# The end of the column projections of a hybrid decoder step: order of work by a readiness clock, key tiles of 256 rows, copies between partition halves

## The chip, the cores and the metric

One core of a Trainium2 chip runs the whole program. The metric is the device time of one execution in microseconds (us); the runs of a version are summed up by their median. Five engines take part, each with its own queue of instructions: TensorE (PE: matmuls and transposes; PEld is its weight load), VectorE (DVE), ScalarE (ACT), GpSimd (POOL) and SyncE (SP), which here issues nearly all DMA transfers. An engine takes its instructions in the order of its queue and waits at an instruction whose inputs or buffers are not ready.

## The reference

One layer of a decoder over a prompt of 1024 rows of width 1024, and one new row for each of 8 samples. One projection feeds three groups of heads, which are gated, joined and projected back:

```python
q_raw, kv_raw, g_raw, z_nsa, u_rw, z_rw, q_mem, z_mem = split_in(rms_norm(hp, ln_g[l]) @ w_in[l])
q, rows4, rows_w = nsa_project(q_raw, kv_raw, pos_p, nsa_q_norm[l], nsa_k_norm[l])
gates = jax.nn.sigmoid(g_raw).reshape(bp, tp, NSA_HEADS, 3)
o_nsa = lax.map(lambda a: nsa_prompt_seq(*a, *cmp_params), (q, rows4, rows_w, gates))
o_rw, sh_p, st_p = rwkv7_mix(u_rw, ...)          # a recurrence over the rows: state S, output y
mkv_p = mem_kv(mem_prompt, mem_norm_g[l], w_mem_kv[l], mem_k_norm[l])   # rms_norm(mem) @ w_kv, 256 rows
o_mem = mem_attend(q_mem, mkv_p, mem_q_norm[l])
hp = hp + mixer_out(o_nsa, z_nsa, o_rw, z_rw, o_mem, z_mem, w_out[l])
```

`nsa_prompt_seq` attends to compressed blocks of keys (made by a small network, `compress`), to selected blocks and to a window, for 8 query heads and 2 key heads of 64. The samples do the same with cached rows. All of it is in float32.

## The kernel before

The program is written in Python that emits one instruction after another; a scheduler then puts every engine's instructions in an order of its own, by the order of emission as priority, by priorities raised with `high_priority`, and by its own model of times. Three tools bind that order. `issue_after(x)` puts an instruction behind x on x's engine. The class `InOrder` (line 72) issues each TensorE instruction after the one before it, so that TensorE's order is the order of emission, and keeps a `clock`, a sum of written costs (0.46 ns a column for a product of float32r, at least 256 columns; 0.11 us a transpose). Its products show up in the profile as line 86 (a helper's line). TensorE instructions on plain `nc.tensor` show their own lines and may be moved by the scheduler.

A float32 product is made of three matmuls, high part by high part, high by low, low by high (`project`, line 298): each weight block is loaded (`wraw`), split by ScalarE into `whi` and by VectorE into `wlo` (two buffers each).

Work before the attention (`phase1`, line 481):

- The columns of `w_in` come in tiles of 128 (`columns`, line 660). Each tile is projected for the rows 0 to 511 with the samples (pieces of 256 and 264) and for the rows 512 to 1023 (one piece of 512): 3 x 24 matmuls. `ORDER` sets their order, the first 17 (`EARLY`) are early columns, the last four are late ones, all of kind z: their result passes ScalarE (tanh) and VectorE (`do_z`, line 309) and is stored to `z_d` by SP.
- The recurrence runs in four chunks of 256 rows (`rwkv_prep`, `rwkv_state`, line 827). Its steps depend on each other; `drive` (line 597) emits as much of the early columns behind each step as the step's `yield` says, as a filler. In `rwkv_state` follow each other: p_x (products of the inverse), its copies W (ScalarE, line 927) and UV (VectorE, line 930), p_g for t = 0 and t = 1 with evictions PT and GT (lines 935 to 949), p_z and p_yy, four steps of p_z and Zn (line 971), and the last part of p_yy. At the end `rwkv_out` makes the rows y and SP stores them (`y_d`, line 1011); `rwkv_close` turns the last state (p_s, line 1017) and SP stores it (line 1021).
- Then `self.pe = nc.tensor`: the late columns are emitted (their matmuls show line 306) and after every 8 of their steps 8 steps of `ahead` (`BG`), which weaves two chains. `attn_keys` (line 1231) loads eight key tiles of 128 rows, each twice side by side (two DMAs of 128 KB, line 1236; the buffer `kd4` has `KB` = 2 turns), turns them by four transposes into PSUM (line 1242, p_k in the profile) and evicts high part (kh, ScalarE, line 1244) and low part (kl, VectorE, line 1245) over all 128 partitions: every key stands on both halves of the partitions, since a query's high part stands on one half and its low part on the other (`q_stack`, line 1292). The values `vs` are loaded in between (line 1238). The other chain is `prompt_cmp` (line 1247: constants, transposes p_xt, the network p_hid and p_co, the turn of the compressed key in `k_split`, line 1190), then `mem_kv` (line 1125): eight groups of two transposes p_mT with evictions mhi and mlo, then the product p_mo (line 1154) in four blocks of 12 matmuls of 512 columns, each with a load and split of `w_mem_kv`; norm and store of the memory's keys and values.

PSUM: the pool `ptr` has two banks (`pM` here), `pw` three, `ppr` three for the columns. `phase2` is the attention; its first scores are p_s<-kh,qs.

Of the kernel before, what the change touches and what calls it, by code (L numbers as in the profile page):

```python
# [26 lines left out]
KB = 2  # L27
# [3 lines left out]
BG = 8  # L31
# [82 lines left out]
class Step:  # L114
# [197 lines left out]
    def do_z(self, H, pieces, row):  # L312
# [6 lines left out]
        nc.sync.dma_start(self.z_d[row:row + 128, H * HALF:H * HALF + HALF], t[:, :HALF])  # L319
# [151 lines left out]
    def phase1(self):  # L471
# [8 lines left out]
        with ExitStack() as ctx:  # L480
# [91 lines left out]
            self.pe = nc.tensor  # L572
# [255 lines left out]
    def rwkv_state(self, Q):  # L828
# [103 lines left out]
        GT, PT = [None] * 2, [None] * 2  # L932
# [23 lines left out]
        yield 0.9  # L956
# [8 lines left out]
        for n in range(4):  # L965
            Zn = self.rc.tile([128, 2, 64], F32, name="Zn", tag="Z", bufs=5)
            for c in range(2):
                for h in range(2):
                    PE.matmul(pz[half[h], n, c, :], PT[n // 2][half[h], c, n % 2, :], Zs[n][half[h], c, :],
# [6 lines left out]
        for t in range(2):  # L976
            for c in range(2):
                for p, h in ((0, 0), (1, 1), (1, 0), (0, 1)):
                    PE.matmul(pyy[h][half[1 - p], t, c, :], GT[t][half[h], c, p, :], Zs[2 * t + p][half[h], c, :],
# [13 lines left out]
    def rwkv_out(self, Q, t, y, yb):  # L993
# [17 lines left out]
        nc.sync.dma_start(self.y_d[r0:r0 + 128, :], yf)  # L1011

    def rwkv_close(self):
        nc, O = self.nc, self.O
        ps = self.pw.tile([128, 2, 128], F32, name="p_s", tag="w")
        for c in range(2):
            nc.tensor.transpose(ps[:64, c, :], self.Z[:, c, :], self.ident[:])
# [15 lines left out]
    def cmp_consts(self):  # L1033

        nc, I = self.nc, self.I
        V, PE = nc.vector, nc.tensor
# [45 lines left out]
    def compress(self, xt, n, hid):  # L1082
# [4 lines left out]
        for e in range(2):  # L1087
# [10 lines left out]
            yield  # L1098

    def cmp_out(self, hid2):  # L1100
# [3 lines left out]
        nc.tensor.matmul(ps[:, :128], hid2, self.w2d[:].rearrange("p a b -> p (a b)"), start=True, stop=True)  # L1104
# [20 lines left out]
    def mem_kv(self):  # L1125
        nc, I, O = self.nc, self.I, self.O
        V, A, PE = nc.vector, nc.scalar, nc.tensor
        xs = self.mem_rows
        his = [self.slot(j, [128, 4, 256], F32R, f"mhi{j}") for j in (4, 0)]
        los = [self.slot(j, [128, 4, 256], F32R, f"mlo{j}") for j in (5, 1)]  # L1130
        for k in range(8):
            ps = self.pM.tile([128, 512], F32, name="p_mT", tag="m")
            for t in range(2):
                PE.transpose(ps[:, t * 128:(t + 1) * 128], xs[t][:, k * 128:(k + 1) * 128], self.ident[:])
            g = self.v("mem_norm_g", k)
# [1380 lines left out]
```

## Time and profile before

| | |
|---|---|
| median of 3 runs | 936.83 us (936.18 to 936.99) |
| the profiled execution | 936.7 us, span 934.9 us |
| TensorE busy | 899.3 us (96%) |
| VectorE, ScalarE, GpSimd busy | 648.0, 434.2, 178.7 us |
| granted clock of TensorE, mean | 0.998 |
| chain that ended last | PE 73%, DVE 17%, ACT 5%, DMA 2%, issue 2% |

A row of the order of time reads: start, duration, engine, line, operation, output<-inputs, shape, count, and in brackets the engine's idle time before it with what ended it. A row of stretches reads: the stretch, its length, then for PE, PEld, DVE, ACT and POOL the busy time with the number of instructions, then the granted clock (1.00 is full), the share of the DMA engines and GB/s (with one line's instructions alone, only the engines that it has). A row of waits reads: who waited for whom, us in total, times, the longest. Matmuls overlap: the distance between starts is what one costs, not its duration.

### The profile page before, as it was taken

To read this page: it belongs to the slowest core of one execution; us is meant where nothing else is said; L and a number is where in the kernel's file an instruction comes from. 1 tells how busy PE (TensorE), PEld (TensorE's weight loads), DVE (VectorE), ACT (ScalarE), POOL (GpSimd) and SP (SyncE) were. 2 spreads that over 40 slices of the span, in tenths; PEclk is the share of its full clock that TensorE was granted. 3 is DMA by queue.
4 is the path that set the end of the run, shared out by engine and by line. 5 is a ranking of instruction groups with operands and counts; after the bars stand their busy time and mean duration, and the time that the engine had idled before them with its cause. 6 is when DMAs were issued, how large, how long until landed. Compare 5 with 4: busy or idle time off the path is not lost.

```text
span 934.9 us, 24813 instructions
## 1 busy us (share of the span) xinstructions
PE 899.3 (96%) x9911; PEld 762.7 (82%) x9911; DVE 648.0 (69%) x2013; ACT 434.2 (46%) x987; POOL 178.7 (19%) x270
## 2 busy tenths in 40 slices
PE   8999999999999999999899999999999999999998
PEld 7998888877878788778777788888887887887976
DVE  7668679864777559946457866765678996548454
ACT  7654324232443234213446666666566766424211
POOL 2000000000000000000104444544344765112010
PEclk9999999999999999999999999999999999999999
DMA  8521313241321205524429313432130036986561
GB/s 278 130 78 35 104 41 105 61 115 48 84 86 52 77 19 143 136 65 132 138 85 275 99 56 108 132 108 60 32 87 10 10 113 168 330 249 218 179 239 47
DMA packets 134698, 105.96 MB, mean 113 GB/s; under 512 B 34641, under 2 KB 120600, under 8 KB 134456
## 3 DMA queue, kind: packets, MB, share of 16 engines
q1 hardware_dynamic: 129592, 92.64, 33.8%
q0 software_dynamic: 3200, 10.49, 3.2%
q8 instruction: 78, 1.28, 0.5%
q10 hardware_dynamic: 1792, 1.26, 0.5%
q14 instruction: 36, 0.29, 0.1%
HBM read 85.77 MB, written 22.78 MB: 116 GB/s over the span
## 4 chain that ended last, share of the span: by engine, by line
PE 73%; DVE 17%; ACT 5%; DMA 2%; issue 2%; POOL 0%; SPq 0%; DVEq 0%; ACTq 0%
PE p_pr L86 20%; PE p_out L86 9%; PE p_pr L306 5%; PE p_o L86 5%; PE p_s L86 5%; PE p_pT L86 5%; PE p_hid L86 3%; ACT p L1416 2%; DVE p L1409 2%; PE p_it L86 1%; PE p_iy L86 1%; PE p_sc L86 1%; DVE pt L1377 1%; DVE wlo L283 1%; PE p_tk L86 1%
## 5 line engine op out<-in xcount | busy, mean ns | idle before, releaser
L86 PE MATMUL p_pr<-h,whi 128*128 128x512 f32 (+2 forms) x976 | 237.0, 336 | 2.0 <-DVE zt L318 2.0
L86 PEld LDWEIGHTS p_pr<-h,whi 128*128 128x128 f32 x976 | 158.6, 189 | 19.5 <-issue 2.4
L86 PE MATMUL p_pr<-h,wlo 128*128 128x512 f32 (+2 forms) x488 | 157.6, 326 | 0.6 <-DVE wlo L283 0.6
L1447 POOL TENSOR_SCALAR p<-p,fac,gates 128x640 f32<-128x640 f32 (+7 forms) x128 | 103.3, 817 | 110.9 <-DVE fac L1443 71.1
L1416 ACT ACTIVATE p<-p,nm 128x640 f32<-128x640 f32 (+7 forms) x128 | 93.1, 728 | 56.3 <-DVE nm L1409 51.3
L86 PEld LDWEIGHTS p_pr<-h,wlo 128*128 128x128 f32 x488 | 91.4, 189 | 9.3 <-DVE wlo L283 0.8
L86 PE MATMUL p_pT<-ident,p 128*128 128x128 f32 x528 | 70.8, 279 | 6.9 <-POOL p L1447 1.9
L1075 POOL MEMSET w2d<- 128x128 f32 x1 | 0.2, 204 | 377.2 <-PE p_iy L86 377.2
L86 PEld LDWEIGHTS p_pT<-ident,p 128*128 128x128 f32 x528 | 56.8, 140 | 18.1 <-issue 6.6
L1409 DVE CUSTOM_DVE_ANT_0 p<-p_s,bmask 128x512 f32<-128x512 f32 (+7 forms) x96 | 60.3, 659 | 16.1 <-PE p_s L86 15.4
L306 PE MATMUL p_pr<-h,whi 128*128 128x264 f32 (+2 forms) x320 | 69.3, 310 | 0.0
L86 PE MATMUL p_o<-pt,vs 128*64 128x128 f32 x1056 | 67.9, 276 | 0.4 <-DVE cat L1485 0.4
L283 DVE TENSOR_TENSOR wlo<-wraw,whi 128x1024 fp32r<-128x1024 f32 x33 | 40.3, 1221 | 36.9 <-ACT whi L282 32.6
L86 PE MATMUL p_s<-kh,qs 128*128 128x512 f32 (+3 forms) x191 | 65.2, 354 | 0.2 <-DVE nm L1409 0.2
L282 ACT ACTIVATE whi<-wraw 128x1024 fp32r<-128x1024 f32 x34 | 36.0, 1059 | 59.6 <-PE p_pr L86 47.1
L86 PEld LDWEIGHTS p_o<-pt,vs 128*64 128x64 f32 x1056 | 57.0, 137 | 7.5 <-issue 3.9
L86 PE MATMUL p_s<-kl,qs 128*128 128x512 f32 (+3 forms) x192 | 60.3, 334 | 0.0
L1377 DVE COPY pt<-p_pT 128x512 f32<-128x512 f32 (+1 forms) x72 | 48.2, 673 | 13.2 <-PE p_pT L86 12.4
L306 PEld LDWEIGHTS p_pr<-h,whi 128*128 128x128 f32 x320 | 51.5, 188 | 3.1 <-issue 0.2
L86 PE MATMUL p_out<-woh,chi 128*128 128x512 f32 x128 | 51.7, 404 | 0.0
L86 PE MATMUL p_out<-woh,clo 128*128 128x512 f32 x128 | 50.2, 392 | 0.4 <-DVE clo L2352 0.4
L86 PE MATMUL p_out<-wol,chi 128*128 128x512 f32 x128 | 49.9, 390 | 0.0
(551 smaller groups left out, 1884.3 us busy)
## 6 DMA issues: line engine op xcount, KB each, us to landing
wraw<-in_w_in_dram SPq DMA_DIRECT2D x34, 512.0 KB
pg<-in_c_pool_dram SPq DMA_DIRECT2D x32, 256.0 KB
pg<-in_c_pool_dram SPq DMA_DIRECT2D x48, 128.0 KB
x<-in_x_prompt_dram SPq DMA_DIRECT2D x8, 512.0 KB
z_d<-zt SPq DMA_DIRECT2D x16, 256.0 KB
cat<-z_d SPq DMA_DIRECT2D x8, 512.0 KB
xres<-in_x_prompt_dram POOLq DMA_DIRECT2D x16, 256.0 KB, 3.8
out_dram<-xres POOLq DMA_DIRECT2D x16, 256.0 KB, 3.0
```

The source lines that it names most:

```text
L86: self.last = getattr(self.engine, op)(*a, **k)
L282: nc.scalar.activation(hi[:, :, :n], raw[:, :, :n], AF.Copy)
L283: (low or nc.vector).tensor_tensor(lo[:, :, :n], raw[:, :, :n], hi[:, :, :n].bitcast(F32), op=OP.subtract)
L306: self.last_mm = self.pe.matmul(ps[:m, :b - a], w[:, k, :m], h[k][:, a:b], start=(k == 0 and i == 0), stop=(k == 7 and i == 2))
L1075: nc.gpsimd.memset(w2d[:], 0.0)
L1377: nc.vector.tensor_copy(pt[:, :n], ps[:, :n])
L1409: return V.tensor_tensor_reduce(halves(x), halves(ps), m, -1.0, 3.0e38, op0=OP.add, op1=OP.min, accum_out=nm[:, h, b:b + 1])
L1416: e = A.activation(x, x, AF.Exp, scale=-1.0, bias=nm[:, h, b:b + 1], accum_out=sm[:, h, b:b + 1])
L1447: nc.gpsimd.tensor_scalar(x, x, f[:, h, b:b + 1], gate[:, hd + h, 1 + b:2 + b], op0=OP.mult, op1=OP.mult)
```

## The change

- The late columns, the recurrence's close, the compression, the key turns and the memory go through one `InOrder` chain on TensorE that starts behind the recurrence's last matmul. A loop `mix` goes through the late columns; after every 1.4 us (`LAG`) of the chain's clock it lets each of two side chains take a step if the time that its last `yield` named has passed.
- The order of the main chain: three late columns, the memory product, the last column. The memory product first runs the second side chain until the memory is turned, and asks for and splits its weights one block ahead.
- Keys: four tiles of 256 rows, loaded once (256 KB each, `KB` = 3, the first three asked for before the loop), turned by four transposes each into a bank of `pw`, evicted half by half into one half of the partitions for each key head. The other halves are filled by eight DMA copies inside SBUF (256 KB each) on SP's queue behind the last z store emitted so far, and the two loads of values (512 KB each) behind these.
- The rows y of the last chunk are stored from GpSimd's queue.
- In `rwkv_state`, in all chunks, p_g is one run of 64 matmuls for both t, with four evictions of 256 elements in place of eight of 128, and the yields 0.9 and 0.9 become one of 1.6.
- The memory is turned in four groups of four transposes, each in one bank.

```diff
-KB = 2
+KB = 3
...
-BG = 8
+LAG = 1.4
...
-            self.pe = nc.tensor
+            self.pe = self.te = InOrder(tc, nc.tensor, self.pe.last)
...
-            bg = self.ahead()
-            late = self.columns(cols[EARLY:])
-            for _ in group(late, 8):
-                for _ in islice(bg, BG):
-                    pass
-            for _ in bg:
-                pass
-    def ahead(self):
-        def keys():
-            for i in range(8):
-                self.attn_keys(i)
-                yield
-            yield from self.q_stack(7)
+            self.mem_turned = False
+            work = [self.keys_ahead(), self.cmp_ahead()]
+            self.mix(work, chain(self.columns(cols[EARLY:-1]), self.mem_product(work[1]), self.columns(cols[-1:])))
+    def keys_ahead(self):
+        rows = self.key_rows
+        yield 5.0
+        for n in range(4):
+            self.turn_keys(n, rows[n])
+            if n == 0:
+                rows.append(self.load_keys(3))
+            yield 2.8
+        yield from self.q_stack(7)
+        with self.tc.issue_after(self.last_z.ins):
+            for h in range(2):
+                self.copy_keys(h)
+        with self.tc.issue_after(self.last_copy.ins):
+            for h in range(2):
+                self.load_values(h)
+    def cmp_ahead(self):
         self.mem_x()
-        yield from weave(chain(self.prompt_cmp(), self.mem_kv()), keys())
+        yield from self.prompt_cmp()
+        yield from self.mem_turn()
+        self.mem_turned = True
+    def mix(self, work, fill):
+        te = self.te
+        ready = {g: te.clock for g in work}
+        while work or fill:
+            for g in list(work):
+                if te.clock >= ready[g] or not fill:
+                    us = next(g, -1)
+                    if us == -1:
+                        work.remove(g)
+                    ready[g] = te.clock + (us or 1.5)
+            start = te.clock
+            while fill and te.clock < start + LAG:
+                if next(fill, None) is None:
+                    fill = None
...
-        for t in range(2):
-            GT[t] = self.rs.tile([128, 2, 2, 64], F32, name="GT", tag=f"GT{t}")
-            PT[t] = self.rs.tile([128, 2, 2, 64], F32, name="PT", tag=f"PT{t}")
-            pgs = [self.pw.tile([128, 4, 64], F32, name="p_g", tag="w") for _ in range(2)]
-            for k in range(2):
+        GT = self.rs.tile([128, 2, 2, 2, 64], F32, name="GT", tag="GT")
+        PT = self.rs.tile([128, 2, 2, 2, 64], F32, name="PT", tag="PT")
+        pgs = [self.pw.tile([128, 2, 4, 64], F32, name="p_g", tag="w") for _ in range(2)]
+        for k in range(2):
+            for t in range(2):
                 for c in range(2):
                     for h in range(2):
                         for pg, o, p in zip(pgs, half, range(2)):
                             x = AM[o, 2 * p + t, 2 * c + h, 64:128] if k else bkT[t][o, c, p, h * 64:h * 64 + 64]
-                            PE.matmul(pg[half[h], 2 * k + c, :], W[t][o, 2 * c + h, :], x, start=True, stop=True)
-            for p, pg in enumerate(pgs):
-                V.tensor_tensor(PT[t][:, :, p, :], pg[:, 0:2], bc(self.eye2[:, None, :], [128, 2, 64]), op=OP.add)
-            for p, pg in enumerate(pgs):
-                V.tensor_tensor(GT[t][:, :, p, :], pg[:, 2:4], ar[:, :, t, 1, p, :], op=OP.add)
-            if t == 0:
-                yield 0.9
+                            PE.matmul(pg[half[h], t, 2 * k + c, :], W[t][o, 2 * c + h, :], x, start=True, stop=True)
+        for p, pg in enumerate(pgs):
+            V.tensor_tensor(PT[:, :, :, p, :], pg[:, :, 0:2], bc(self.eye2[:, None, None, :], [128, 2, 2, 64]), op=OP.add)
+        for p, pg in enumerate(pgs):
+            V.tensor_tensor(GT[:, :, :, p, :], pg[:, :, 2:4], ar[:, :, :, 1, p, :].rearrange("p c t e -> p t c e"), op=OP.add)
...
-        yield 0.9
+        yield 1.6
...
-        nc.sync.dma_start(self.y_d[r0:r0 + 128, :], yf)
+        (nc.gpsimd if Q == 3 else nc.sync).dma_start(self.y_d[r0:r0 + 128, :], yf)
...
+    def mem_product(self, turns):
+        nc, O = self.nc, self.O
+        A, PE = nc.scalar, self.te
+        while not self.mem_turned:
+            next(turns, None)
+        his, los = self.mem_hi, self.mem_lo
         po = [self.pw.tile([128, 512], F32, name="p_mo", tag="w") for t in range(2)]
+        w = self.mem_block(0)
         for k in range(0, 8, 2):
-            raw = self.wr.tile([128, 2, 512], F32, name="wraw")
-            nc.sync.dma_start(raw[:], I["w_mem_kv"][0, k * 128:(k + 2) * 128, :].rearrange("(k p) c -> p k c", p=128))
-            wh = self.wp.tile([128, 2, 512], F32R, name="whi")
-            wl = self.wp.tile([128, 2, 512], F32R, name="wlo")
-            A.activation(wh[:], raw[:], AF.Copy)
-            V.tensor_tensor(wl[:], raw[:], wh[:].bitcast(F32), op=OP.subtract)
-            yield
+            (wh, wl), w = w, self.mem_block(k + 2) if k < 6 else None
             for j in range(2):
                 for t in range(2):
                     cs = slice(t * 128, (t + 1) * 128)
                     h, l = his[k // 4][:, (k + j) % 4, cs], los[k // 4][:, (k + j) % 4, cs]
-                    for i, (a, w) in enumerate(((h, wh), (h, wl), (l, wh))):
-                        PE.matmul(po[t][:], a, w[:, j], start=(k + j == 0 and i == 0), stop=(k + j == 7 and i == 2))
-            yield
+                    for i, (a, b) in enumerate(((h, wh), (h, wl), (l, wh))):
+                        PE.matmul(po[t][:], a, b[:, j], start=(k + j == 0 and i == 0), stop=(k + j == 7 and i == 2))
+                    yield STEP
...
+        self.key_rows = [self.load_keys(n) for n in range(3)]
...
-    def attn_keys(self, i, tag="m"):
-        nc = self.nc
-        A, G = nc.scalar, nc.gpsimd
-        kk = self.kt.tile([128, 4, 2, 64], F32, name="kd4", tag="kd4", bufs=KB)
-        for s in range(2):
-            nc.sync.dma_start(kk[:, :, s, :], self.k_d[i * 128:(i + 1) * 128, :].rearrange("t (j d) -> t j d", d=64))
-        if i % 4 == 0:
-            nc.sync.dma_start(self.vs[i // 4][:].rearrange("p k b g d -> p k (b g d)"),
-                              self.v_d[i * 128:(i + 4) * 128, :].rearrange("(k p) c -> p k c", p=128))
-        ps = self.pM.tile([128, 4, 128], F32, name="p_k4", tag=tag)
-        for j in range(4):
-            nc.tensor.transpose(ps[:, j, :], kk[:, j].rearrange("p s d -> p (s d)"), self.ident[:])
-        kh, kl = (x[i // 4][:, :, i % 4 * 128:i % 4 * 128 + 128] for x in (self.kh, self.kl))
-        A.activation(kh, ps[:], AF.Copy)
-        nc.vector.tensor_tensor(kl, ps[:], kh.bitcast(F32), op=OP.subtract)
+    def load_keys(self, n):
+        kk = self.kt.tile([128, 2, 2, 128], F32, name="kd4", tag="kd4", bufs=KB)
+        self.nc.sync.dma_start(kk[:].rearrange("p i j d -> p i (j d)"),
+                               self.k_d[n * 256:(n + 1) * 256, :].rearrange("(i p) c -> p i c", p=128))
+        return kk
+    def turn_keys(self, n, kk):
+        nc = self.nc
+        ps = self.pw.tile([128, 2, 2, 128], F32, name="p_k4", tag="w")
+        for j in range(2):
+            for i in range(2):
+                self.te.transpose(ps[:, j, i, :], kk[:, i, j], self.ident[:])
+        c = slice(n % 2 * 256, n % 2 * 256 + 256)
+        for g in range(2):
+            o = slice(g * 64, g * 64 + 64)
+            x = ps[o].rearrange("p j i t -> p j (i t)")
+            kh, kl = self.kh[n // 2][o, g::2, c], self.kl[n // 2][o, g::2, c]
+            self.exp = nc.scalar.activation(kh, x, AF.Copy)
+            nc.vector.tensor_tensor(kl, x, kh.bitcast(F32), op=OP.subtract)
+    def copy_keys(self, h):
+        for x in (self.kh[h], self.kl[h]):
+            for g in range(2):
+                o, to = slice(g * 64, g * 64 + 64), slice(64 - g * 64, 128 - g * 64)
+                self.last_copy = self.nc.sync.dma_start(x[to, g::2].bitcast(F32), x[o, g::2].bitcast(F32))
+    def load_values(self, h):
+        self.nc.sync.dma_start(self.vs[h][:].rearrange("p k b g d -> p k (b g d)"),
+                               self.v_d[h * 512:(h + 1) * 512, :].rearrange("(k p) c -> p k c", p=128))
```

`yield` of `compress` becomes 3.0, of `prompt_cmp` 4.0 before its constants, 6.0 behind p_co and 4.0 at its end, and `mem_turn` yields 2.8 after each group; the first query stack (`q_stack(7)`) is put behind the last key eviction on ScalarE.

More of the change, by code (lines that the diff above doesn't have):

```diff
@@ L318, in do_z @@
             nc.vector.scalar_tensor_tensor(t[:, a:b], t[:, a:b], 1.0, ps[:, :b - a], op0=OP.add, op1=OP.mult)
[L319 removed]
+        self.last_z = nc.sync.dma_start(self.z_d[row:row + 128, H * HALF:H * HALF + HALF], t[:, :HALF])
         if H == 0:
@@ L968, in rwkv_state @@
                 for h in range(2):
-                    PE.matmul(pz[half[h], n, c, :], PT[n // 2][half[h], c, n % 2, :], Zs[n][half[h], c, :],
+                    PE.matmul(pz[half[h], n, c, :], PT[half[h], n // 2, c, n % 2, :], Zs[n][half[h], c, :],
                               start=False, stop=True, skip_group_check=True)
@@ L978, in rwkv_state @@
                 for p, h in ((0, 0), (1, 1), (1, 0), (0, 1)):
-                    PE.matmul(pyy[h][half[1 - p], t, c, :], GT[t][half[h], c, p, :], Zs[2 * t + p][half[h], c, :],
+                    PE.matmul(pyy[h][half[1 - p], t, c, :], GT[half[h], t, c, p, :], Zs[2 * t + p][half[h], c, :],
                               start=False, stop=(c == 1), skip_group_check=True)
@@ L1016, in rwkv_close @@
         for c in range(2):
-            nc.tensor.transpose(ps[:64, c, :], self.Z[:, c, :], self.ident[:])
+            self.te.transpose(ps[:64, c, :], self.Z[:, c, :], self.ident[:])
         S = self.rs.tile([64, 2, 128], F32, name="S_out", tag="W0")
@@ L1103, in cmp_out @@
         ps = self.pM.tile([128, 512], F32, name="p_co", tag="m")
-        nc.tensor.matmul(ps[:, :128], hid2, self.w2d[:].rearrange("p a b -> p (a b)"), start=True, stop=True)
+        self.te.matmul(ps[:, :128], hid2, self.w2d[:].rearrange("p a b -> p (a b)"), start=True, stop=True)
         c = self.wk.tile([128, 2, 64], F32, name="c_o", tag="c_o")
@@ L1123, in mem_x, with mem_turn @@
             xs.append(x)
-    def mem_kv(self):
-        nc, I, O = self.nc, self.I, self.O
-        V, A, PE = nc.vector, nc.scalar, nc.tensor
+    def mem_turn(self):
+        nc = self.nc
+        V, A, PE = nc.vector, nc.scalar, self.te
         xs = self.mem_rows
[L1129 to L1135, printed above, removed]
-            hi, lo = his[k // 4][:, k % 4, :], los[k // 4][:, k % 4, :]
-            A.activation(hi, ps[:, :256], AF.Copy, scale=g)
-            V.scalar_tensor_tensor(lo, ps[:, :256], g, hi.bitcast(F32), op0=OP.mult, op1=OP.subtract)
-            yield
+        his = self.mem_hi = [self.slot(j, [128, 4, 256], F32R, f"mhi{j}") for j in (4, 0)]
+        los = self.mem_lo = [self.slot(j, [128, 4, 256], F32R, f"mlo{j}") for j in (5, 1)]
+        for k0 in range(0, 8, 2):
+            ps = self.pM.tile([128, 2, 256], F32, name="p_mT", tag="m")
+            for k in (k0, k0 + 1):
+                for t in range(2):
+                    PE.transpose(ps[:, k % 2, t * 128:(t + 1) * 128], xs[t][:, k * 128:(k + 1) * 128], self.ident[:])
+            for k in (k0, k0 + 1):
+                g = self.v("mem_norm_g", k)
+                hi, lo = his[k // 4][:, k % 4, :], los[k // 4][:, k % 4, :]
+                A.activation(hi, ps[:, k % 2], AF.Copy, scale=g)
+                V.scalar_tensor_tensor(lo, ps[:, k % 2], g, hi.bitcast(F32), op0=OP.mult, op1=OP.subtract)
+            yield 2.8
@@ new lines, in mem_block @@
+    def mem_block(self, k):
+        nc, I = self.nc, self.I
+        raw = self.wr.tile([128, 2, 512], F32, name="wraw")
+        nc.sync.dma_start(raw[:], I["w_mem_kv"][0, k * 128:(k + 2) * 128, :].rearrange("(k p) c -> p k c", p=128))
+        wh = self.wp.tile([128, 2, 512], F32R, name="whi")
+        wl = self.wp.tile([128, 2, 512], F32R, name="wlo")
+        nc.scalar.activation(wh[:], raw[:], AF.Copy)
+        nc.vector.tensor_tensor(wl[:], raw[:], wh[:].bitcast(F32), op=OP.subtract)
+        return wh, wl
@@ L1301, in q_stack @@
             hl = pool.tile([128, 4, 2, 64], F32R, name="qhl", tag=tag, bufs=nb)
-            with self.tc.issue_after(self.exp.ins) if i == 6 else ExitStack():
+            with self.tc.issue_after(self.exp.ins) if i > 5 else ExitStack():
                 A.activation(hl[:, :, 0], q[:, 4 * b:4 * b + 4], AF.Copy)
```

14 lines of the change are left out of this document (6 added, 8 removed).

## Prediction

> **What bounds the kernel now.** I read the page first, then the busy time by stretch, the waits of TensorE, and the order of time around the places that the change touches.
>
> ```profile
> span 934.9 us, 24813 instructions
> PE 899.3 (96%) x9911; PEld 762.7 (82%) x9911; DVE 648.0 (69%) x2013; ACT 434.2 (46%) x987; POOL 178.7 (19%) x270
> ```
>
> TensorE (PE) is busy 96% of the span, so a change pays only by taking work from TensorE or by closing its gaps; 35.6 us of gaps exist in all. The stage that the change rewrites, the columns' end, runs from the turn of the last state (p_s) to the first attention score. Two stretches of TensorE, the tail of the recurrence and this stage:
>
> ```profile
> 420.79:496.62 75.83, 71.14 (x460) 59.33 (x459) 41.72 (x148) 29.10 (x63) 3.19 (x6) 1.00 0.45 126
> 407.72:420.79 13.07, 12.87 (x262) 11.45 (x260) 5.50 (x20) 1.70 (x6) 0.00 (x0) 1.00 0.20 55
> ```
>
> The first number after the length is TensorE: in the stage it idles 75.83 - 71.14 = 4.7 us, in the tail before it 0.2 us. The waits of TensorE in the stage:
>
> ```profile
> PE p_k L1242 <- DMA kd<-k_d: 2.4, 2, 1.9
> PE p_mo L1154 <- DVE wlo L1147: 0.5, 1, 0.5
> PE p_k L1190 <- POOL kd L1183: 0.5, 1, 0.5
> PE p_pr L306 <- DVE wlo L283: 0.4, 2, 0.2
> PE p_k L1242 <- issue: 0.4, 1, 0.4
> PE p_k L1242 <- DVE kl L1245: 0.3, 1, 0.3
> ```
>
> More than half of it is key tiles that have not landed. So the most that closing gaps can bring is 4.7 us, and the rest must come from work taken away.
>
> **Keys: removed.** Now eight tiles are turned by four transposes each (32); afterwards four tiles by four (16), and the other half of the partitions is filled by copies. A group of four takes from one start to the next:
>
> ```profile
> 441.85 0.60 PE L1242 MATMUL p_k<-ident,kd 128*128 128x128 f32 x4
> 442.28 0.60 PE L1275 MATMUL p_xt<-ident,px 128*128 128x128 f32 x4
> ```
>
> 0.43 us, so 16 fewer save 4 x 0.43 = 1.7 us. The evictions don't shrink: eight on ScalarE and eight on VectorE of 512 elements a partition before and after. The key loads stand today behind the stores of the recurrence on SyncE's queue (SP):
>
> ```profile
> 421.89 2.44 SPq L1021 DMA_DIRECT2D out_dram<-S_out  x4
> ...
> 427.85 1.97 SPq L1011 DMA_DIRECT2D y_d<-y_c  x2
> 429.91 1.26 SPq L1236 DMA_DIRECT2D kd<-k_d  x2
> ...
> 433.85 0.63 PE L1242 MATMUL p_k<-ident,kd 128*128 128x128 f32 x4 [0.59 <-DMA kd<-k_d]
> ...
> 448.44 0.63 PE L1242 MATMUL p_k<-ident,kd 128*128 128x128 f32 x4 [1.86 <-DMA kd<-k_d]
> ```
>
> With the y stores on GpSimd's queue (idle there) and three tiles of space over rows that columns no longer use, three loads can go by the end of the state stores at the latest, near 424. The first turn comes 6 us of column work into the stage. From load to use took 3.9 us above (429.91 to 433.85), so it is there. I take the whole 2.4 us of load waits and the 0.3 us for a buffer (turns move to the pool of three): 2.7 us. If the state's stores come late, the first wait (0.6) stays.
>
> The turn of the compressed key waits for GpSimd, and the memory's transposes stand in pairs between products:
>
> ```profile
> 460.85 0.46 PE L1104 MATMUL p_co<-w2d,phid 128*128 128x128 f32 x2
> ...
> 466.31 0.33 PE L1190 MATMUL p_k<-ident,kd 128*128 128x128 f32 x1 [0.49 <-POOL kd L1183]
> ...
> 469.74 0.48 PE L1154 MATMUL p_mo<-whi,mlo 128*128 128x512 f32 x1
> 470.06 0.40 PE L1154 MATMUL p_mo<-whi,mhi 128*128 128x512 f32 x1
> 470.30 0.40 PE L1154 MATMUL p_mo<-wlo,mhi 128*128 128x512 f32 x1
> ```
>
> The key's turn comes 5.5 us after p_co with 0.5 us of wait; the change leaves 6.0 us of its own clock between them: -0.5 us. A product behind a pair of transposes takes 0.32 us to the next one, the following 0.24: 0.08 for each return. The eight pairs become one run, seven returns fewer: 0.6 us. Removed in all: 1.7 + 2.7 + 0.5 + 0.6 = 5.5 us.
>
> **The tail of the recurrence: added.** This is what speaks against the change. Today the late columns are issued on plain TensorE, so the scheduler may slide their products (line 306) up between the last steps of the recurrence, and it does:
>
> ```profile
> 407.72:420.79 13.07, 4.80 (x27) 3.56 (x27) 1.00 0.20 55
> ...
> 429.79 0.28 PE L306 MATMUL p_pr<-h,wlo 128*128 128x256 f32 x1
> ...
> 430.15 0.28 PE L306 MATMUL p_pr<-h,wlo 128*128 128x256 f32 x1
> ```
>
> 27 products of a late column stand there, since the early columns are used up. Afterwards every late product is chained behind the last matmul of the recurrence, so nothing fills the tail, and the 27 come later: from one low-part product to the next, with two others between, 0.36 us pass (429.79 to 430.15), so 9 x 0.36 = 3.2 us. In return the tail gets shorter, since its steps no longer stand behind a filler. Its steps:
>
> ```profile
> 410.34 0.38 ACT L927 ACTIVATE W<-p_x 128x256 f32<-128x256 f32 x1 [0.78 <-PE p_x L86]
> 410.76 1.75 DVE L930 COPY UV<-p_x 64x256 f32<-64x256 f32 x4 [0.82 <-ACT W L927]
> ...
> 414.63 1.15 PE L86 MATMUL p_z<-UV,bkT 128*64 128x64 f32 x32
> ...
> 416.74 0.45 PE L86 MATMUL p_z<-Zn,PT 64*64 64x64 f32 x8
> ...
> 417.23 0.29 DVE L971 TENSOR_TENSOR Zn<-p_z,gC 128x128 f32<-128x128 f32 x1 [1.61 <-PE p_z L86]
> ...
> 417.79 0.45 PE L86 MATMUL p_z<-Zn,PT 64*64 64x64 f32 x8
> ...
> 420.79 0.41 PE L1017 MATMUL p_s<-ident,Zn 128*64 128x128 f32 x2
> ```
>
> Of 13.07 us, 4.80 are filler and 0.2 idle: 8.1 us of its own. Waits that open: p_g on the first copies out of p_x, about 0.7 (two of 0.44); p_yy on the merged evictions of p_g (four of 0.44, the time of a UV copy with as many elements, and 0.1, less the 1.15 of p_z), 0.7; and three Zn steps, each 0.78 from p_z to the end of Zn plus some 0.1 less the 0.38 of p_z, 1.5. The tail becomes 8.1 + 2.9 = 11.0 us, 2.1 shorter; net cost 3.2 - 2.1 = **1.1 us**. Bounds: -0.3 if only the Zn waits open (8.1 + 1.5 against 13.07 - 3.2), +3.2 if the tail stays as long as it is. I take 1.1, since the Zn rows give its largest part.
>
> In the first three chunks of the recurrence the merge of p_g spares one interruption of the filler and VectorE four instructions each; filler hides the rest. At 0.08 us a return and some hand-over I take -0.3 us (-0.6 to +0.6).
>
> **The memory turns: added.** Following the change's own clock through its loop (0.24 us for a product of 512 columns, 0.11 for a transpose, 1.4 between looks), the three columns end at 43 us while the chain of compression has just reached the turn of its key. The memory product must not start before the memory is turned, so it pulls all four groups of turns without a column between them. They go through two PSUM buffers, each emptied twice by ScalarE and twice by VectorE:
>
> ```profile
> 469.43 1.07 ACT L1137 ACTIVATE mhi<-p_mT,vec 128x256 fp32r<-128x256 f32 x2 [0.45 <-PE p_mT L1134]
> ...
> 469.93 1.08 DVE L1138 SCALAR_TENSOR_TENSOR mlo<-p_mT,vec,mhi 128x256 fp32r<-128x256 f32 x2 [0.44 <-ACT mhi L1137]
> ```
>
> One group so needs 4 x 0.53 = 2.1 us if the two engines take turns on it, as W and UV do on p_x above (410.34 + 0.38, then 410.76). The third group waits 2.1 less the 0.43 of the second, the fourth another 1.0 (two evictions of the other bank) less 0.43: **2.3 us**. Bounds: 0.7 if both engines read side by side, 3.8 if the split of a weight block (below) goes between. What hides this now is the memory product, between whose matmuls the turns stand.
>
> **Copies, values, weights.** Eight copies of 256 KB and two loads of 512 KB go out about 29 us into the stage, 45 us before the first score. The nearest row of a rate, and the weights' own path:
>
> ```profile
> 500.00:510.00 10.00, 8.23 (x50) 6.14 (x50) 9.12 (x23) 8.47 (x18) 5.71 (x7) 1.00 0.98 284
> ...
> 479.61 0.38 SPq L274 DMA_DIRECT2D wraw<-in_w_in_dram  x1
> ...
> 483.52 1.06 ACT L282 ACTIVATE whi<-wraw 128x1024 fp32r<-128x1024 f32 x1 [3.61 <-DMA wraw<-in_w_in_dram]
> ...
> 484.61 1.23 DVE L283 TENSOR_TENSOR wlo<-wraw,whi 128x1024 fp32r<-128x1024 f32 x1 [3.30 <-ACT whi L282]
> ```
>
> At 284 GB/s 3 MB take 11 us, at a quarter of it 44. No copy inside the chip is in this trace; I cost them at nothing, hidden by the last two columns and the memory product (without that cover, the first score waits for what is left). Of the weights a split takes 1.06 + 1.23 = 2.3 us, the twelve matmuls of a block 12 x 0.24 = 2.9: it fits by 0.6. I keep the 0.9 us of wlo waits of now.
>
> **The clock.** One gap of TensorE is dearer than its length:
>
> ```profile
> 275.24 0.73 PE L86 MATMUL p_pr<-h,whi 128*128 128x512 f32 x2 [1.96 <-DVE zt L318]
> ...
> 275.00:280.00 5.00, 4.76 (x14) 3.77 (x15) 1.26 (x5) 0.00 (x0) 0.00 (x0) 0.66 0.45 158
> ```
>
> After a wait of 1.96 us the granted clock was 0.66 over 5 us: 1.7 us lost. The wait of 1.86 us at 448.44 cost no clock (1.00 in the stage). The new waits are below 1.7 us each, so I add nothing. The Trainium skill, "TensorE: Matmul & The Clock Gate", section "HAM oscillation — how this bites in real kernels", puts the limit at idle gaps over about 3.4 us; the trace shows a drop at 1.96, and the measurement decides. By that page of the Trainium skill the sum is the same as mine.
>
> By the row at 275 a gap that grows to 2 us would add 1.7.
>
> **Sum.** -5.5 + 1.1 - 0.3 + 2.3 = -2.4 us. The profiled execution took 936.7 us (span 934.9), the median of the runs 936.83: the same. Forecast 936.7 - 2.4 = **934.3 us**, own range 932 to 936.5.
>
> **Rivals.**
> - More is gained. The wait at 275 (1.96 us and 1.7 us of clock) hangs on VectorE's queue in the third chunk; earlier chunks have fewer VectorE instructions afterwards, and a different order there can drop it: 934.3 - 3.7 = 930.6. Against it: it is far from the edit. The same size comes if the memory turns overlap fully and the tail costs nothing. Chance 0.20.
> - Nothing comes of it: the tail keeps its length, 3.2 in place of 1.1, so 936.4. For it: the chain of VectorE and TensorE there is one long dependence. Chance 0.12.
> - A new gap reaches 2 us and halves the clock for a while: 934.3 + 1.7 = 936.0. Chance 0.06.
> - Slower: the memory product runs at the pace of its loads. Its matmuls are now one unbroken run in a fixed order, with two raw buffers, and the copies (2 MB) and values go through the same queue just before. A block whose load is asked for only when its turn comes takes 3.9 (479.61 to 483.52) + 2.3 = 6.2 us in place of 2.9: 3.3 us for each late block. One late block gives 937.6, two 940.9. It decides if the third block's load is issued later than the start of the first block's matmuls. Chance 0.17.
> - The forecast: 0.45.
>
> **How the numbers follow.** A measurement here tells about 0.2%, 1.9 us, from no change: the line lies at 934.9. Of the forecast's 0.45, 0.28 lies below it and 0.17 above; with the first rival faster is 0.48; 0.17 + 0.12 + 0.06 = 0.35 is the same; slower 0.17. The range 930.5 to 938.5 takes in the first rival's time and one late block; it leaves out some 0.06 below and 0.10 above.
>
> **What would show it.** Right: no wait of a key turn for a load; 16 key transposes; between p_x and p_s no column product, with gaps of about 0.5 us at the Zn steps, and p_s near 419; four groups of memory turns in a row with gaps summing to 2 us or more just before the first p_mo; first score near 494. Wrong: a p_mo or the last column's product waiting on wraw; scores waiting for a copy; a clock below 1.00 in the stage; or a stage before 400 us whose length moves by over 1 us.

## The result, and the profile after

The changed kernel takes 945.25 us (median of 6 runs, 941.19 to 947.93); the kernel before took 936.91 beside it (6 runs, 935.37 to 941.94). The ratio is 1.0081, 95% interval 1.0054 to 1.0108: slower, by more than any case of the prediction and in a direction that it gave 0.17. The profiled run of the change took 941.19 us, 4.5 us above that of the kernel before.

The page of the changed kernel begins:

```profile
span 939.4 us, 24746 instructions
PE 897.5 (96%) x9895; PEld 764.6 (81%) x9895; DVE 646.5 (69%) x1997; ACT 434.0 (46%) x987; POOL 179.9 (19%) x272
```

TensorE is busy 1.8 us less, while the span is 4.5 us longer. Busy time by stretch of the changed kernel (after the length come PE, PEld, DVE, ACT, POOL, each with its instructions, then the granted clock of TensorE, the DMA share and GB/s); the first two are from p_x to the turn of the last state, and from there to the first score:

```profile
408.13:417.78 9.65, 7.84 (x226) 6.89 (x225) 4.71 (x14) 1.02 (x3) 0.00 (x0) 1.00 0.18 67
417.78:501.40 83.62, 74.09 (x472) 64.14 (x469) 42.31 (x149) 29.74 (x64) 5.55 (x11) 0.94 0.45 125
425.00:430.00 5.00, 0.43 (x2) 0.47 (x3) 2.34 (x9) 0.00 (x0) 2.52 (x5) 0.79 0.71 198
430.00:435.00 5.00, 5.00 (x43) 3.31 (x42) 2.52 (x6) 1.18 (x2) 0.00 (x0) 0.52 0.57 199
470.00:475.00 5.00, 2.18 (x14) 1.47 (x12) 2.54 (x5) 2.71 (x6) 0.03 (x1) 1.00 0.29 45
475.00:480.00 5.00, 3.98 (x15) 3.22 (x16) 3.11 (x7) 2.57 (x6) 0.00 (x0) 0.66 0.41 149
```

From p_x to the turn of the state the kernel before took 11.59 us:

```profile
409.20:420.79 11.59, 11.39 (x249) 10.01 (x248) 5.29 (x19) 1.40 (x4) 0.00 (x0) 1.00 0.11 32
```

That part is 1.94 us shorter now. The stage was 75.83 us long and is now 83.62; TensorE idles 83.62 - 74.09 = 9.5 us in it, after 4.7. The third number from the end is the new thing: a mean clock of 0.94 where it was 1.00, from two holes. From 425 to 430 TensorE does almost nothing, and from 430 to 435 it is busy all the time at little over half speed; a smaller hole with a low clock behind it follows at 470 to 480. Its waits in the stage and the tail:

```profile
PE p_k L86 <- DMA kd<-k_d: 5.3, 1, 5.3
PE p_mT L86 <- DVE ckl L1226: 2.5, 1, 2.5
PE p_mT L86 <- DVE mlo L1161: 1.4, 2, 0.9
PE p_z L86 <- DVE Zn L992: 1.2, 3, 0.4
PE p_g L86 <- DVE UV L954: 0.5, 1, 0.5
```

The last two are the tail's, 1.2 and 0.5 us where 1.5 and 0.7 were forecast; the 0.7 of p_yy did not open. The first is a wait that was to vanish. The order of time around both holes (rows picked out):

```profile
418.93 2.44 SPq L1042 DMA_DIRECT2D out_dram<-S_out  x4
425.30 0.34 SPq L319 DMA_DIRECT2D z_d<-zt  x1
425.45 0.72 POOL L1032 DMA_DIRECT2D y_d<-y_c  x1 [21.36 <-DVE rq_t L135]
425.68 0.43 SPq L321 DMA_DIRECT2D z_d<-zt  x1
426.16 1.51 SPq L1269 DMA_DIRECT2D kd<-k_d  x3
427.47 0.55 POOL L1032 DMA_DIRECT2D y_d<-y_c  x1 [1.29 <-DVE y_c L1030]
428.01 1.08 POOL L1304 MEMSET bmask<- 128x1152 bf16 x1
429.12 0.23 DVE L1306 CAST bmask<-c_am 128x128 bf16<-128x128 f32 x1 [2.00 <-POOL bmask L1304]
429.56 1.09 PE L86 MATMUL p_k<-ident,kd 128*128 128x128 f32 x4 [5.26 <-DMA kd<-k_d]
...
470.83 1.06 ACT L1170 ACTIVATE whi<-wraw 128x1024 fp32r<-128x1024 f32 x1 [4.42 <-issue]
471.92 1.22 DVE L1171 TENSOR_TENSOR wlo<-wraw,whi 128x1024 fp32r<-128x1024 f32 x1 [2.47 <-ACT whi L1170]
473.66 0.28 DVE L1226 TENSOR_TENSOR ckl<-p_k,ckh 128x128 fp32r<-128x128 f32 x1
474.00 0.66 PE L86 MATMUL p_mT<-ident,mx 128*128 128x128 f32 x4 [2.47 <-DVE ckl L1226]
475.50 0.90 PE L86 MATMUL p_mT<-ident,mx 128*128 128x128 f32 x4 [0.85 <-DVE mlo L1161]
476.92 1.09 PE L86 MATMUL p_mT<-ident,mx 128*128 128x128 f32 x4 [0.51 <-DVE mlo L1161]
```

The state's stores are out by 421.4, and then SyncE's queue stands still for four microseconds: next on it is the z store of the first late column, which waits for VectorE's last eviction of that column. Only behind that pair of stores do the three key loads leave, at 426.16. TensorE's fixed order has arrived at the first key turn by 424.3 (429.56 - 5.26) and may not pass it. At 470 the memory's turns come in one run, as forecast, with 2.47 + 0.85 + 0.51 = 3.8 us of waits. The longest of them is not a memory group's wait for the one before it: the second group needs the bank in which the compressed key was turned, and that bank is free only behind the key's low part (ckl, 473.66), which stands on VectorE behind the split of a weight block (whi, wlo).

For what follows each run's time is taken apart in two: the **lost clock**, the span times what the mean granted clock lacks to 1, and the **full-clock time**, the rest. (Low clock in an idle stretch is counted as lost too, though it costs nothing there, and the waits are in the full-clock time.) In 35 runs of the kernel before, taken beside some of the experiments, the time lies between 933.47 and 942.18, and its full-clock time is 933.7 with a deviation of 0.6: nearly all of the scatter is clock.

| kernel | runs | median us | mean clock | lost us | full-clock us |
|---|---|---|---|---|---|
| before | 35 | 937.85 | 0.9956 | 4.1 | 933.7 |
| the change | 6 | 945.25 | 0.9885 | 10.9 | 934.2 |

(Lost and full-clock are means over the runs; the mean's error is 0.4 and 0.1 us before, 1.2 and 0.4 after.) So the change is 0.5 us slower at full clock and loses 6.8 us more by clock. The 0.5 is what is left of two things that nearly cancel, as the profiles show from p_x to the first score. That part takes 93.27 us (9.65 + 83.62) where it took 87.42 (11.59 + 75.83): 5.9 more, where the sum had -5.5 + 1.1 + 2.3 = -2.1. Idle time in it rose from 4.9 to 11.3 us, by 6.4. The clock there costs up to some 5 us (83.62 x 0.06), less what fell into the holes. So TensorE's work at full clock must have fallen, by some 5 us as well. The work was saved; new waits used it up, and the clock behind them made the change the slower of the two.

The experiments ran in three sets, each with the kernel before beside it: 29 runs with e1, e2, e12 and e123 (median 937.92 us, full-clock 933.2), the 35 with warm, b_store, b_merge and e5 (937.85, 933.7), and 19 with e8, e9 and e6 (938.12, 934.2). So a difference of under 1 us between versions of different sets tells nothing.

### The profile page after: what moved, and what is told of

The parts are those of the page before. It is cut to its first block, busy times and chain, and to the rows that moved or that the text cites. A ratio compares the mean times of both kernels' runs of the same rounds, so it can differ in the third digit from the quotient of the medians.

```text
span 939.4 us, 24746 instructions
## 1 busy us (share of the span) xinstructions
PE 897.5 (96%) x9895; PEld 764.6 (81%) x9895; DVE 646.5 (69%) x1997; ACT 434.0 (46%) x987; POOL 179.9 (19%) x272
## 3 DMA queue, kind: packets, MB, share of 16 engines
q8 instruction: 78, 1.28, 0.6%
## 4 chain that ended last, share of the span: by engine, by line
PE 68%; DVE 18%; ACT 6%; issue 4%; DMA 2%; POOL 0%; SPq 0%; ACTq 0%; DVEq 0%; POOLq 0%
PE p_pr L86 22%; PE p_out L86 9%; PE p_o L86 5%; PE p_s L86 5%; PE p_pT L86 4%; PE p_hid L86 3%; ACT p L1469 3%; PE p_pr L306 2%; DVE p L1462 2%; PE p_sc L86 1%; DVE pt L1430 1%; PE p_it L86 1%; PE p_tk L86 1%; PE p_iy L86 1%; DVE wlo L283 1%
## 5 line engine op out<-in xcount | busy, mean ns | idle before, releaser
L86 PE MATMUL p_pr<-h,whi 128*128 128x512 f32 (+2 forms) x1168 | 281.0, 334 | 2.0 <-DVE zt L318 2.0
L86 PEld LDWEIGHTS p_pr<-h,whi 128*128 128x128 f32 x1168 | 189.9, 189 | 22.2 <-issue 2.8
L86 PE MATMUL p_pr<-h,wlo 128*128 128x512 f32 (+2 forms) x584 | 188.3, 325 | 0.8 <-DVE wlo L283 0.8
L86 PEld LDWEIGHTS p_pr<-h,wlo 128*128 128x128 f32 x584 | 109.7, 189 | 11.0 <-DVE wlo L283 1.2
L1428 ACT ACTIVATE pt<-p_pT 128x512 f32<-128x512 f32 (+1 forms) x72 | 41.2, 578 | 17.7 <-PE p_pT L86 17.0
L86 PEld LDWEIGHTS p_s<-kh,qs 128*128 128x128 f32 x191 | 36.2, 189 | 3.2 <-DVE nm L1462 0.8
```

Source lines behind the costliest of these rows:

```text
L86: self.last = getattr(self.engine, op)(*a, **k)
L1428: nc.scalar.activation(pt[:, :n], ps[:, :n], AF.Copy)
```

## The experiments

The theory after this comparison: the key loads stand on SyncE's queue behind a z store, the memory's turns come in a run, and each hole costs its length and then a stretch of half clock. The rivals: the tail without filler carries the loss; the key tiles' space and not their place in the queue holds the loads; a hole's length is its whole price.

**The key loads ahead of the z stores (e1).** The z stores are issued behind the third key load:

```diff
+        with self.tc.issue_after(self.key_load.ins) if self.key_load else ExitStack():
-        self.last_z = nc.sync.dma_start(self.z_d[...], t[:, :HALF])
+            self.last_z = nc.sync.dma_start(self.z_d[...], t[:, :HALF])
```

> Only the order on SyncE's queue changes: the z stores of the late columns are issued behind the first three key loads. Theory (queue order): the loads leave right behind the state's stores, near 419 to 422, the first key turn's wait falls from 5.26 us to under 1 us, the clock between 425 and 435 stays near 1.00 (0.79 and 0.52 after the change); 4.5 us of wait and 2.4 to 3.4 us of clock come back, so about 7 us below the changed kernel: 934 to 938, by the profiled run of the change. Rival (space): the key tiles lie over rows that a column still uses, so the loads leave at 426 again with a wait near 5 us, and the time is that of the changed kernel. Rival (the tail without filler is the loss): the wait goes but under 2 us of the time does.

940.33 us, 1.0034 times the kernel before (1.0015 to 1.0054); lost 7.8, full-clock 932.8. The order of time:

```profile
420.96 1.61 SPq L1271 DMA_DIRECT2D kd<-k_d  x3
...
423.92 0.63 PE L86 MATMUL p_k<-ident,kd 128*128 128x128 f32 x4
...
424.83 0.33 SPq L320 DMA_DIRECT2D z_d<-zt  x1
...
432.22 0.47 PE L86 MATMUL p_pt<-pe_s,pe_c 128*128 128x4 f32 x2 [3.25 <-DVE pe_c L1081]
```

The loads leave at 420.96 and the first key turn waits for nothing: it was the queue's order, and the space is there. But of the 7 us only 5 came back, since a new wait of 3.25 us opened a little further on, for the bias rows (pe_c) on VectorE, with a mean clock of 0.74 from 430 to 435. The long wait had hidden it.

**The memory's turns among the columns (e2), and both (e12).**

```diff
         ck, cv = self.cmp_out(...)
-        yield 6.0
+        yield from self.mem_turn()
+        self.mem_turned = True
         self.k_stack(ck, 1, self.ckh[:], self.ckl[:])
```

> Only the memory's turns move: they stand among the columns, between the compressed key and its turn, in place of one forced run before the memory product. Theory: 3.8 us of idle time at the turns and about 1.7 us of clock between 475 and 480 go; the first key turn's wait of 5 us stays; 3.5 to 5.5 us below the changed kernel. Rival (the turns' waits are only moved: their two PSUM buffers are shared with the compression's products): under 1.5 us.

943.53 us, 1.0065 (1.0041 to 1.0089); lost 10.8, full-clock 932.5. Against the change that is 1.7 us less, and no less clock lost: near the rival. The columns still ended before the turns did, so the last two groups came in one run, and the compressed key's turn behind them waited 3.4 us for their evictions (mlo).

> Both of the above. Theory: the two losses are independent, so the gains add: 10 to 12 us below the changed kernel, some 929 to 934, thus below the kernel before. Rival (the tail without filler, or copies and values beside the columns, carry the loss): at or above the kernel before, 936 or more.

938.91 us, 1.0019 (1.0000 to 1.0038); lost 6.4, full-clock 933.0: 6 us below the change, not the 10 to 12 of the theory, and level with the kernel before. Two waits of TensorE hold what is left:

```profile
PE p_k L86 <- DVE mlo L1161: 3.4, 1, 3.4
PE p_pt L86 <- DVE pe_c L1079: 3.2, 1, 3.2
```

**Filler back in the tail (e123).** As e12, with the first late column counted among the early ones (EARLY + 1 in the fill and in the mix).

> Both of the above, and the first late column goes to the early ones, so that the recurrence's last steps have its products between them again. Theory (the tail's net cost is about 1 us): 0.5 to 1.5 us below the run without this. Rival (the tail is a main part of the loss): 3 us or more below it. It may also show nothing if the column is used up in an earlier part of the recurrence.

944.77 us, 1.0089 (1.0061 to 1.0118): 6 us slower than e12, which neither theory expected. Busy time by stretch, then waits:

```profile
407.00:420.00 13.00, 13.00 (x231) 11.85 (x229) 4.62 (x14) 1.40 (x4) 0.00 (x0) 1.00 0.14 52
420.00:500.00 80.00, 68.56 (x457) 58.73 (x457) 40.08 (x143) 29.59 (x63) 5.56 (x11) 0.89 0.42 122
```

```profile
PE p_k L86 <- DMA kd<-k_d: 3.6, 1, 3.6
PE p_k L86 <- POOL kd L1217: 3.3, 1, 3.3
PE p_co L86 <- ACT c_th L1116: 2.3, 1, 2.3
PE p_mT L86 <- DVE rq_t L132: 2.0, 1, 2.0
```

The tail is filled to the brim, and the columns' end starves: 11.4 us of idle time, a clock of 0.89. So a column is worth far more as cover for the turns than as filler in the tail. What the tail without filler costs by itself this run does not show: its full-clock time (932.2 us, 933.0 in e12) holds the new waits, and the clock that it leaves out was in part low in idle time (0.50 all the way from 469.5 to 482.5, with the waits of 2.0 and 3.3 us in it).

**A hole filled with useless work (warm).** The changed kernel with 46 transposes of the identity ahead of the first key turn:

```diff
         ps = self.pw.tile([128, 2, 2, 128], F32, name="p_k4", tag="w")
+        for _ in range(46 if n == 0 else 0):
+            self.te._do("transpose", ps[:, 0, 0, :], self.ident[:], self.ident[:])
```

> The changed kernel with 46 extra transposes of the identity (0.11 us each, 5.0 us) put on TensorE just ahead of the first key turn, in the bank that this turn then overwrites: work that nobody needs, in the place of the 5.26 us gap. Theory (an idle gap costs its length and then the halved clock behind it): the gap shrinks to under 1 us, the clock between 425 and 435 is 1.00 in the profile, the mean granted clock rises by about 0.003, and the time falls by 2 to 3.5 us though no wait has become shorter. Rival (the gap's length is the whole price): the same time as the changed kernel within 1 us, or longer.

941.41 us, 1.0033 (1.0014 to 1.0051): 3.8 us less than the change, by work that nobody needs. Order of time, then the two stretches that stood at 0.79 and 0.52:

```profile
423.68 5.18 PE L86 MATMUL p_k<-ident 128*128 128x128 f32 x46
...
429.25 0.66 PE L86 MATMUL p_k<-ident,kd 128*128 128x128 f32 x4 [0.39 <-DMA kd<-k_d]
```

```profile
425.00:430.00 5.00, 4.62 (x48) 4.21 (x50) 1.89 (x7) 0.06 (x1) 2.49 (x5) 1.00 0.69 217
430.00:435.00 5.00, 5.00 (x53) 4.07 (x46) 2.88 (x9) 1.71 (x3) 0.00 (x0) 1.00 0.48 178
```

The key turn starts at 429.25 in place of 429.56, and the clock stays at 1.00. Lost falls from 10.9 to 5.7 us, full-clock time rises by 1.4 (the low clock inside the idle hole had been counted as lost). That the hole's clock, apart from its length, was a large part of the loss is shown.

**Parts of the change in the kernel before (b_store, b_merge).** The y stores on GpSimd's queue alone, and the merged p_g alone; the edits are the change's own lines.

> The kernel before with one part of the change: the last y stores leave on GpSimd's queue. By the prediction's step: the key loads leave earlier, the 2.4 us of waits for key tiles shrink below 1 us, 1 to 2 us faster, 935 to 936.5. Rival (the key loads are held by their two buffers, not by the y stores): only the first wait (0.6 us) goes, no difference that can be measured.

> The kernel before with another part alone: the merged p_g and its evictions in all four chunks of the recurrence. By the prediction's step: -0.3 us (-0.6 to +0.6), nothing that can be measured. Rival (the merge moves waits into the recurrence and with them the clock): 2 us or more slower, with a lower mean clock and a drop before 400 us.

937.82 us for the stores (0.9999, 0.9978 to 1.0020), the waits for key tiles 1.5 us in place of 2.4; 938.22 for the merge (1.0008, 0.9988 to 1.0027), with a lost clock of 4.1 us, as before. Neither part by itself makes a difference in time that can be told. The rival on the merge falls. On the stores the waits went the prediction's way in part, and the full-clock time is 932.7 +- 0.2 against 933.7 +- 0.1, so some 1 us was gained; the clock (5.2 us lost, 4.1 in the kernel before) hid it.

**More room, first try (e5).** As e12, with the bias rows' turn 4 us later and the last column ahead of the memory product.

> Queue order and memory turns as in the run with both, and two more waits of TensorE's fixed order taken away: the turn of the bias rows is asked for 4 us of column work later (a wait of 3.2 us for VectorE there), and the last column goes ahead of the memory product, so that the turns still have columns between them (a wait of 3.4 us there). Theory (what remains of the loss is gaps that a fixed order of TensorE makes, and their clock): no gap over 1.5 us between 405 and 500 but for the tail's, 6 us less than the run with both, some 931 to 934, and a mean clock as high as that of the kernel before (0.995 or more). Rival (the operands are late whatever the order): the waits appear at the next products, and the time stays at 937 to 939.

939.45 us, 1.0015 (0.9994 to 1.0037); lost 7.6, full-clock 931.6. The two waits went, and three others came: 2.3 us of the first query turn for GpSimd, 0.7 for a weight, 3.2 of the second block of scores, since the memory product's norm and evictions now stood on VectorE just when the scores needed it. The rival's outcome; that column had been there as cover.

**The memset behind the y stores (e8).** In the kernel before the block mask was cleared on GpSimd long before it was wanted:

```profile
404.62 1.05 POOL L1252 MEMSET bmask<- 128x1152 bf16 x1
```

In the change it stands behind the y stores that wait for the last y (425.45, 427.47) and comes at 428.01. As e12, and:

```diff
-        G.memset(self.bmask[:], 0.0)
+        V.memset(self.bmask[:], 0.0)
```

> Queue order and memory turns as in the run with both; in addition one memset (the block mask's) goes from GpSimd to VectorE. In the changed kernel this memset stands on GpSimd behind the two y stores (428.01 in place of 404.62), VectorE waits 2.00 us for it, and the bias rows that TensorE waits for stand behind that on VectorE. Theory (the y stores block GpSimd, and through it VectorE and TensorE): the mask's wait on VectorE goes, the wait of p_pt for VectorE falls from 3.2 us to about 1.2, some 2 us less at full clock, and a smaller chance of a lost clock: 935 to 938. Rival (the two engines taking turns on the key tile's bank set the time of the bias rows): p_pt waits 2.5 us or more as before, and the time is that of the run with both.

938.12 us, 1.0021 (0.9998 to 1.0043); full-clock 931.6, which is 2.7 below the kernel before beside it, where e12 was 0.2 below its own. The order of time:

```profile
427.77 0.54 DVE L1306 MEMSET bmask<- 128x576 uint32 x1
428.37 0.32 DVE L1308 CAST bmask<-c_am 128x128 bf16<-128x128 f32 x1
...
431.95 0.39 PE L86 MATMUL p_pt<-pe_s,pe_c 128*128 128x4 f32 x2 [1.64 <-DVE pe_c L1079]
```

VectorE's wait of 2.00 us is gone and the bias rows' wait is 1.64 in place of 3.20: half of it came through GpSimd. In time that gain cannot be told from the clock's scatter (lost 7.4 after 6.4).

**Room for all three waits (e9, e6).** e9 is e8 with pauses in the fixed order; e6 leaves the memset on GpSimd and gives the bias rows 4.0 and 3.0:

```diff
             V.tensor_copy(pc[32 * g:32 * g + 2, :], rows[g])
-        yield
+        yield 3.0
         yield
...
         self.mem_turned = True
+        yield 3.0
+        yield 3.0
         self.k_stack(ck, 1, self.ckh[:], self.ckl[:])
...
+            if first and b == 0:
+                yield 4.0
             ps = self.pM.tile([128, 4, 128], F32, name="p_q", tag="m")
```

> As the run with the mask's memset moved, and the three waits of TensorE that are left are given room in its fixed order: the bias rows' turn 1.5 us of column work later, the first query turn 4 us later, the compressed key's turn some 4 us into the memory product. Theory (the loss is gaps made by the fixed order): no gap over 1 us between 420 and 490, about 5 us less at full clock than the run with queue order and memory turns alone, 930 to 935, below the kernel before. Rival (operands late whatever the order): new waits of the same sum at the next products, 937 or more.

> As the last, but the mask's memset stays on GpSimd behind the y stores, and the bias rows' turn gets 4 us of room in its place. Theory: as good as the last within 1.5 us, 931 to 936, since it matters only that TensorE has work until the operand is there. Rival (VectorE's lost 2 us are themselves on the path): 2 us or more above the last.

e9: 929.15 us (6 runs, 927.50 to 931.25), 0.9908 times the kernel before (0.9879 to 0.9937); lost 3.4, full-clock 925.9. e6: 930.90 us, 0.9927 (0.9902 to 0.9952); lost 5.0, full-clock 926.0. Tail and stage of e9, and its waits of TensorE from 405 to 500 that sum to 0.5 us or more:

```profile
410.39:420.04 9.65, 7.85 (x226) 6.89 (x225) 4.71 (x14) 1.02 (x3) 0.00 (x0) 1.00 0.17 61
420.04:490.77 70.73, 69.85 (x473) 61.69 (x470) 42.19 (x150) 29.44 (x64) 4.63 (x10) 1.00 0.53 143
```

```profile
PE p_z L86 <- DVE Zn L992: 1.2, 3, 0.4
PE p_s L86 <- DVE nm L1469: 0.6, 2, 0.4
PE p_mT L86 <- DVE mlo L1161: 0.6, 1, 0.6
PE p_g L86 <- DVE UV L954: 0.5, 1, 0.5
```

The same work in the same tiles takes 70.73 us in place of 83.62, with 0.9 us of idle time in place of 9.5 and a clock of 1.00. This version beats both kernels. In time e6 is 1.75 us above e9, where 1.5 was the most expected; all of that is clock (5.0 lost, 3.4 in e9). That e6 is as good at full clock shows that a late operand is no harm as long as TensorE's order holds other work until it is there.

## Why the prediction was wrong

- **The clock: the step that failed worst.** "The wait of 1.86 us at 448.44 cost no clock (1.00 in the stage). The new waits are below 1.7 us each, so I add nothing." Two things were wrong. The new waits were up to 5.26 us. And I drew a limit between 1.96 us and 1.86 from one execution, in which the one gap was followed by half clock and the other not. There is no such line: in b_store and b_merge the clock fell behind a gap of 1.88 us near 384, and in the kernel before it did not behind one of 1.86 at 383 (more in the last section). Measured: 6.8 us more lost clock, of which filling one hole gave back 5.1 +- 1.2. The rival "a new gap reaches 2 us" had the mechanism, with one hole at 1.7 us and a chance of 0.06; there were two holes, one followed by 7 us of half clock.
- **The key loads: failed.** "Three loads can go by the end of the state stores at the latest, near 424 ... so it is there." I moved the loads past the y stores on SyncE's queue and overlooked what else is queued there: the z stores of the column that now runs at the same time. In place of 2.7 us gained the wait grew from 2.4 to 5.3. Undone in e1, the loads left at 420.96.
- **GpSimd's queue: failed, hidden.** I called it idle, and named what the y stores would leave, not what they would hold up. The mask's memset stood behind them, VectorE behind that, TensorE behind VectorE: 1.6 us of e12's 3.2 us wait. In the changed kernel itself the key hole covered it.
- **The memory turns: mechanism right in part, size at its bound.** The waits that were forecast, of the third group and the fourth, took 0.85 + 0.51 = 1.4 us in place of 2.3. The other 2.47 us, of the second group for the bank of the compressed key, were not in the sum. That the total of 3.8 meets the bound is partly luck, though its condition came true: the split of a weight block went ahead of that key's eviction.
- **The tail: right in length, partly by luck.** It was to become 2.1 us shorter and became 1.94 shorter (9.65 after 11.59). But its waits are 9.65 - 7.84 = 1.8 us in place of 2.9, so its own work must be about as much longer than the 8.1 assumed. The 3.2 us for the products moved out of it were not measured apart, so the net 1.1 is not shown.
- **The rest: right.** The key turns need half the transposes, and TensorE's work fell at least as far as forecast; the p_g merge cannot be told from nothing (b_merge); no score waited for a copy; the rival that was to make it slower did not come, since no p_mo waited for a weight.

What the wrong steps share: before, the late columns were on plain TensorE and the scheduler placed them; the change put every instruction of TensorE there in one chain, so an operand that is later than the chain assumes becomes a hole, and, as e1 and e12 show, one hole hides the next. My terms cost each wait as it stood in the trace of before, where the order could give way. With room made for three operands the gain is 9.0 us (938.12 - 929.15), 8.4 of it at full clock, more than the -2.4 of the sum. By the profiles, from p_x to the first score, 7.0 us of it stand there (87.42 to 9.65 + 70.73 = 80.38), with a clock of 1.00 in both: 4.8 us less work of TensorE (82.53 to 77.70) and 2.2 less idle time (4.9 to 2.7). The forecast's own terms for less work there come to 3.9: 1.7 for the transposes, 0.6 for the returns, and 4.80 - 3.2 = 1.6 for the late products that no longer stand between other steps. They were not measured apart; the other 0.9, and the 1.4 us of gain outside this part, stay open.

## What to carry to other kernels

When a change makes an engine's order fixed, list every instruction in that order with the engine or queue that makes its operand, and give each the room that its chain needs; the first hole will hide the others, so expect a second and a third. A load that is moved ahead on a queue is only as early as the last store that still stands before it, and a store that is moved to an idle engine holds up whatever that engine did next. Price a hole of TensorE at its length plus the expected clock behind it, and read the clock from several executions, not from one.

## What was not expected of the hardware

Whether a gap halves the clock is not settled by its length. In the thirteen profiled kernels TensorE waits 1.96 to 1.98 us near 274 for the same eviction; in six of them half clock followed, in seven not. Here is one of each, e12 and then the change, each with its order of time and then its stretch behind the gap:

```profile
273.88 1.08 PE L86 MATMUL p_pr<-h,whi 128*128 128x512 f32 x2 [1.96 <-DVE zt L318]
```

```profile
275.00:278.00 3.00, 3.00 (x9) 2.32 (x9) 0.00 (x0) 0.00 (x0) 0.00 (x0) 0.59 0.48 176
```

```profile
274.54 0.73 PE L86 MATMUL p_pr<-h,whi 128*128 128x512 f32 x2 [1.97 <-DVE zt L318]
```

```profile
275.00:278.00 3.00, 3.00 (x15) 2.42 (x14) 0.57 (x2) 0.00 (x0) 0.00 (x0) 1.00 0.71 241
```

Behind another gap, of 1.27 or 1.28 us near 320, the clock fell in nine of the thirteen. Even a gap of 0.89 us near 700, in the attention, had half clock some 2.5 us behind it in four of them (in e2 the gap ends at 705.02, and the clock is 0.50 from 708 to 714). Of fourteen gaps from 2.3 to 5.3 us, after the start of the kernels, that began at full clock twelve were followed by half clock; one of 3.41 us in e12 was not, while the gap of the same length at the same place in e2 and e8 was. Read in steps of 1 us, the low stretches last about 3.4 us or twice that (1.7 or 3.4 us lost); one in e123, with two more gaps inside it, lasts over 13. The Trainium skill, "TensorE: Matmul & The Clock Gate", section "Part 1: The HAM clock gate", says that activity is watched in a window of about 3.4 us that runs freely and does not start anew with the kernel. The length of the low stretches and the chance in them agree with that. The limit that the Trainium skill gives on the same page, section "HAM oscillation — how this bites in real kernels", idle gaps over about 3.4 us, does not agree: low stretches followed gaps of 1.28 and 1.97 us.
